# A transformer kernel's first block: who makes the low parts of the weights, and which queue carries the bias tables

## The chip, the core and the metric

The kernel runs on one core of a Trainium2 chip. The metric is the time of one execution in device microseconds (us). A core has TensorE (PE, matrix products), VectorE (DVE), ScalarE (ACT), GpSimd (POOL) and SyncE (SP); each takes its own instructions strictly in their order, and semaphores tie the engines together. Transfers (DMAs) are issued from an engine's queue, and the issuing engine goes on while the data moves.

## What is computed

Two transformer blocks follow each other on a sequence of 512 tokens with 1024 features. All sizes below are of the first block's mixer, which is where the change lies.

```
h = rms_norm(x, norm1_g);  z = h @ w_in
z_pool, s_b, s_c, s_h, c_a, c_g, zq, zk, zv = split(z)
y_pool  = pool_mixer(z_pool)                      # sliding means, then a 64x64 product per group
y_sconv = s_b * causal_dwconv(s_c * s_h)          # 3 taps
u       = causal_dwconv(c_a * sigmoid(c_g)) + b   # 31 taps
y_conf  = silu(layer_norm(u))
y_attn  = diff_attention(zq, zk, zv, rel_bias)    # 4 heads, softmax twice, difference by lambda
x = x + concat(y_pool, y_sconv, y_conf, y_attn) @ w_out
x = x + (silu(h2 @ w_gate) * (h2 @ w_up)) @ w_down
```

Lambda comes from four vectors of 32 numbers: exp(sum(lq1*lk1)) - exp(sum(lq2*lk2)) + a constant. The second block has two more layers with other mixers; its attention uses a second table of relative biases.

## The kernel before

**Products in two parts.** Every large product is made from float32 values that are cut in a high and a low part: `hi` is a rounded copy, `lo = value - hi`. Three products are added up (hi*hi, hi*lo, lo*hi). For activations `feed` (L209 to L220) makes the parts. For weights it is `weights` (from L108): it loads 128x1024 numbers into `wraw` (two buffers) from SyncE's queue (L119), ScalarE casts each half to `whi` (L129), and the engine in `self.lo` subtracts to `wlo` (L130); there are four buffers each of `whi` and `wlo`. L144 (`f_acc`) holds the matmuls with features as output rows, L163 (`t_proj`) those with tokens as output rows. `setup` puts VectorE into `self.lo` (L308); `layer1`, after the first four units of weights, puts GpSimd there (L441), and `run` puts VectorE back after the first block (L1347). In a stretch of the second block (L777 to L856) GpSimd makes lo parts as well; the change leaves that alone.

**The order.** A planner orders the instructions of each engine ahead of time, by priority and by its own estimates. Work under `first()` goes ahead of ordinary work, work under `chain()` ahead of most. The order on each engine is then fixed. A generator list (`bg`) mixes the attention's steps into the matmuls of the projections.

**The first block, in program order.** `setup` (L305) loads the input and constants. `layer1` (L381) makes the parts of the activations and the norm, then calls `tables` (L347): two small matmuls turn the relative biases into rows `t1` (4x640) and `t2` (8x656), and two DMAs write each row 32 times into tables in main memory (`tab1`, `tab2`; L369 and L370). The staging tiles (one-hot rows, mask row, `t1`, `t2`) live in a pool that is closed at the end of `tables`. The memory is then given to the block's own pool, `l1`, and a tile that lies over an older one waits for that one's last user. From SyncE's queue also come the meta rows of `x` (L372), the constants `cs1` (L406), the bias tile `B1` in four pieces read from `tab1` with a shift for each row (`sheared`, L374 to L378), and the pool weights (L413).

Then follow: lambda and scaled gains (L415 to L429, small VectorE instructions and one exponential); the projection `cg` and its sigmoid; the projection `ca`; the product `u = ca * sigmoid(cg)` on VectorE (L444) behind 30 zeros (a memset on GpSimd, L434); the token projections v, k, q (L549 evacuates them on ScalarE); per tile of 128 tokens a chain of norm, split and transposes for k and q (`heads`, L458 to L478, in which VectorE, ScalarE and TensorE alternate); the attention's `logits` (L491 to L502, in which VectorE adds `B1`), `turn`, `values` and `finish`; and the convolution: two VectorE instructions start `y` (L559), 60 more add a tap each (L561). The convolution has ordinary priority. Afterwards come the projections for pooling and the short convolution (L566 to L599), the layer norm of the convolution's result (L608 to L631), and the output product in two halves, the first with the pooling and short convolution, the second with the long convolution and the attention.

Of the kernel before, what the change touches and what calls it, by code (L numbers as in the profile page):

```python
# [8 lines left out]
F32 = mybir.dt.float32  # L9
# [48 lines left out]
class Kern:  # L58
# [246 lines left out]
    def setup(self):  # L305
# [34 lines left out]
            nc.vector.tensor_copy(self.bf[n], self.ident if n == "ident" else k(n))  # L340
        self.m1 = m1

        ps = self.ch("a")
        for _ in range(10):
            nc.tensor.matmul(ps[:, :128], lhsT=m1, rhs=m1, start=True, stop=True)

    def tables(self):  # L347

        nc, io = self.nc, self.io
        self.tab1 = self.dram.tile([4, COPIES, N1], F32, name="tab1")  # L350
        self.tab2 = self.dram.tile([8, COPIES, N2], F32, name="tab2")
        with self.tc.tile_pool(name="setup", bufs=1) as p:
            oh = p.tile([32, N1 + N2], F32, name="oh")
            nc.sync.dma_start(oh, io["onehot"])
            mrow = p.tile([4, N1], F32, name="mrow")
            nc.sync.dma_start(mrow, io["mrow"])
            rb = p.tile([32, 12], F32, name="relb")
            nc.sync.dma_start(rb, io["relb"])
            t1 = p.tile([4, N1], F32, name="t1")
            t2 = p.tile([8, N2], F32, name="t2")  # L360
            for c0, c1 in ((0, 512), (512, N1)):
                ps = self.ch("a")
                nc.tensor.matmul(ps[:4, :c1 - c0], lhsT=rb[:, 0:4], rhs=oh[:, c0:c1], start=True, stop=True)
                nc.vector.tensor_tensor(out=t1[:, c0:c1], in0=ps[:4, :c1 - c0], in1=mrow[:, c0:c1], op=OP.add)
            for c0, c1 in ((0, 512), (512, N2)):
                ps = self.ch("a")
                nc.tensor.matmul(ps[:8, :c1 - c0], lhsT=rb[:, 4:12], rhs=oh[:, N1 + c0:N1 + c1], start=True, stop=True)
                nc.vector.tensor_copy(t2[:, c0:c1], ps[:8, :c1 - c0])
            nc.sync.dma_start(self.tab1, t1[:, None, :].to_broadcast([4, COPIES, N1]))  # L369
            nc.sync.dma_start(self.tab2, t2[:, None, :].to_broadcast([8, COPIES, N2]))  # L370
            for k in range(KT):
                nc.sync.dma_start(self.x[k][:, 0:M], io["meta"][k])  # L372

    def sheared(self, out, tab, n):  # L374

        for p0 in range(0, 128, COPIES):
            src = bass.AP(tensor=tab.tensor, offset=tab.offset + 127 - p0, ap=[[n - 1, COPIES], [COPIES * n, out.shape[1]], [1, out.shape[2]]])
            self.nc.sync.dma_start(out[p0:p0 + COPIES], src)  # L378


    def layer1(self):  # L381
# [10 lines left out]
        with tc.tile_pool(name="l1", bufs=1, reuse_waits="tile") as p:  # L392
# [4 lines left out]
            def fproj(out):  # L397
                for f in range(2):
# [3 lines left out]
                    with self.first():  # L402
                        nc.vector.tensor_tensor(out=out[:, f], in0=ps, in1=rbx, op=OP.mult)

            cs = p.tile([128, NCS1], F32, name="cs1")
            nc.sync.dma_start(cs, self.io["cs1"])  # L406
            B1 = p.tile([128, 4, S], F32, name="B1")
            self.sheared(B1, self.tab1, N1)
            pw = p.tile([128, 2, 128], F32, name="pw")
            nc.gpsimd.memset(pw, 0.0)  # L410
            for g in range(4):
                o = g % 2 * 64
                nc.sync.dma_start(pw[o:o + 64, g // 2, o:o + 64], self.io["pool_w"][g])  # L413

            rp = lambda n: self.rowp[:, ROWS[n][0]:ROWS[n][0] + ROWS[n][1]]  # L415
            lam = p.tile([128, 4], F32, name="lam")
            lt = p.tile([128, 32], F32, name="lt")
            for i in (1, 2):
                nc.vector.tensor_tensor(out=lt, in0=rp(f"lq{i}"), in1=rp(f"lk{i}"), op=OP.mult)
                nc.vector.tensor_reduce(lam[:, i:i + 1], lt, axis=AX.X, op=OP.add)  # L420
            nc.scalar.activation(lam[:, 1:3], lam[:, 1:3], AF.Exp)

            nc.vector.tensor_tensor(out=lam[:, 0:1], in0=lam[:, 2:3], in1=lam[:, 1:2], op=OP.subtract)
            lam_init = 0.8 - 0.6 * math.exp(-0.3 * 0)
            nc.vector.tensor_scalar(lam[:, 0:1], lam[:, 0:1], -lam_init, None, op0=OP.add)
            gq = p.tile([128, 32], F32, name="gq")
            nc.vector.scalar_tensor_tensor(gq, rp("qg"), 32 ** -0.5, rp("kg"), op0=OP.mult, op1=OP.mult)
            gs = p.tile([128, 64], F32, name="gs")
            nc.vector.tensor_scalar(gs, rp("sub"), 1.0 - lam_init, None, op0=OP.mult)  # L429


            PADC = 30
            u = p.tile([128, 2, PADC + S], F32, name="u")
            nc.gpsimd.memset(u[:, :, :PADC], 0.0)  # L434
            ca, cg = X2(S), X2(S)
            fproj(cg)
            with self.chain():
                for f in range(2):
                    self.sigmoid(cg[:, f], cg[:, f])
            fproj(ca)  # L440
            self.lo = nc.gpsimd  # L441
            with self.chain():
                for f in range(2):
                    nc.vector.tensor_tensor(out=u[:, f, PADC:], in0=ca[:, f], in1=cg[:, f], op=OP.mult)  # L444
# [2 lines left out]
            tiles = [(M + 128 * t, 128) for t in range(4)]  # L447
            flat = lambda t: t.rearrange("p f t -> p (f t)").rearrange("p (t c) -> p t c", t=4)
            qt, kt, vt = (flat(G(S, n)) for n in ("qtok", "ktok", "vtok"))
            qT, kT = (p.tile([128, 8, S], F32R, name=n) for n in ("qT", "kT"))  # L450
            yT = G(S, "yT")

            def heads(i, src, dst, b):
# [109 lines left out]

            PADP = 16
            z = G(PADP + S, "z", "ktok")
            nc.gpsimd.memset(z[:, :, :PADP], 0.0)  # L566
            fproj(z[:, :, PADP:])

            PADS = 2
            sb, sc, sh = G(S, "sb", "qtok"), X2(PADS + S), X2(S)  # L570
            nc.gpsimd.memset(sc[:, :, :PADS], 0.0)
            fproj(sc[:, :, PADS:])
            fproj(sh)
            fproj(sb)
# [958 lines left out]
```

## Time and profile before

| | |
|---|---|
| time, median of 3 runs | 1260.43 us (1259.63 to 1261.51) |
| the profiled execution | 1260.34 us, span 1258.5 us |
| TensorE busy | 1212.1 us (96%) |
| VectorE busy | 813.2 us (65%) |
| ScalarE busy | 616.5 us (49%) |
| GpSimd busy | 134.5 us (11%) |
| granted TensorE clock | 0.988 |
| lo parts of weights on VectorE (L130) | 280, 666 ns each in the mean |
| lo parts of weights on GpSimd (L130) | 70, 1382 ns each in the mean |
| taps of the convolution (L561) | 60, 910 ns each in the mean |

In the profile's rows an instruction stands as engine, line, operation, what it writes and reads, its shape and count. A bracket tells how long the engine was idle just before, and what ended the idle time. "Busy" counts instructions only; time in a queue's waits is idle time. TensorE's ends are modelled and overlap a little, so two matmuls of 0.39 us can start 0.23 us apart.

### The profile page before, as it was taken

The numbers are of one execution on the slowest core, as the hardware profiler recorded it, in microseconds if no ns is written. First come the engines' busy times: TensorE is split into PE (matmuls) and PEld (weight loads), VectorE is DVE, ScalarE is ACT, GpSimd is POOL, SyncE is SP. The second block draws the span as 40 slices with busy tenths as digits, with TensorE's granted clock in tenths as the row PEclk, the third lists the DMA queues.
The fourth block names the chain that finished last, engine by engine and source line by source line (L and its number), as shares of the span: only waits on it lengthen the run. The fifth ranks groups of instructions, "written<-read, shape, count | busy, mean of one in ns | idle before, by whom it ended". The sixth has DMA issues, their size and how long they took to land.

```text
span 1258.5 us, 19045 instructions
## 1 busy us (share of the span) xinstructions
PE 1212.1 (96%) x7242; PEld 1023.7 (81%) x7242; DVE 813.2 (65%) x1816; ACT 616.5 (49%) x1367; POOL 134.5 (11%) x108
## 2 busy tenths in 40 slices
PE   8968999999999999999989999999999999999996
PEld 6966767888888888887888889899899989886776
DVE  6499986544433444454498989666566476685675
ACT  5356645433322333344444435666554484575754
POOL 0433336100000000013322000000010000000000
PEclk9989999999999999999998999999999999999999
DMA  6531112233223323233211212222223223120121
GB/s 190 122 80 54 51 51 75 93 100 100 78 90 113 101 89 101 80 92 124 88 51 51 62 49 71 81 69 68 69 68 118 84 68 93 60 82 20 51 67 68
DMA packets 34736, 101.44 MB, mean 81 GB/s; under 512 B 5536, under 2 KB 7984, under 8 KB 34644
## 3 DMA queue, kind: packets, MB, share of 16 engines
q1 hardware_dynamic: 32836, 98.06, 25.7%
q10 hardware_dynamic: 1808, 2.16, 0.5%
q8 instruction: 57, 0.93, 0.3%
q14 instruction: 35, 0.29, 0.1%
HBM read 96.03 MB, written 3.10 MB: 79 GB/s over the span
## 4 chain that ended last, share of the span: by engine, by line
PE 78%; DVE 16%; ACT 2%; DMA 2%; issue 1%; POOL 0%; SPq 0%; DVEq 0%; ACTq 0%; POOLq 0%
PE mm L144 64%; DVE y L561 3%; PE psb L174 3%; DVE sc L817 2%; DVE sc L827 1%; PE pso L1218 1%; DMA tab<-t 1%; DVE m L826 1%; PE pso L971 1%; DVE e L493 1%; DVE mx L103 1%; PE psa L1099 1%; DVE e L502 1%; PE pso L973 1%; DVE wlo L130 1%
## 5 line engine op out<-in xcount | busy, mean ns | idle before, releaser
L144 PE MATMUL mm<-hhi,whi 128*128 128x512 f32 (+3 forms) x1296 | 444.8, 344 | 1.7 <-ACT whi L129 1.6
L144 PE MATMUL mm<-hhi,wlo 128*128 128x512 f32 (+3 forms) x1296 | 437.9, 338 | 0.1
L144 PE MATMUL mm<-hlo,whi 128*128 128x512 f32 (+3 forms) x1296 | 436.2, 337 | 0.2 <-DVE hlo L217 0.2
L129 ACT CAST whi<-wraw 128x512 fp32r<-128x512 f32 x350 | 207.4, 595 | 335.9 <-PE mm L144 289.3
L130 DVE TENSOR_TENSOR wlo<-wraw,whi 128x512 fp32r<-128x512 f32 (+2 forms) x280 | 185.9, 666 | 144.2 <-ACT whi L129 116.8
L144 PEld LDWEIGHTS mm<-hhi,whi 128*128 128x128 f32 (+1 forms) x1296 | 246.0, 190 | 28.1 <-ACT whi L129 2.3
L144 PEld LDWEIGHTS mm<-hhi,wlo 128*128 128x128 f32 (+1 forms) x1296 | 245.7, 190 | 26.7 <-issue 1.2
L144 PEld LDWEIGHTS mm<-hlo,whi 128*128 128x128 f32 (+1 forms) x1296 | 246.0, 190 | 25.6 <-DVE hlo L217 1.5
L130 POOL TENSOR_TENSOR wlo<-wraw,whi 128x512 fp32r<-128x512 f32 (+1 forms) x70 | 96.3, 1382 | 181.9 <-ACT whi L129 171.9
L144 PE MATMUL mm<-mx,whi 128*128 128x512 f32 (+2 forms) x448 | 112.2, 338 | 2.0 <-DVE mx L103 1.6
L231 POOL TENSOR_TENSOR acc<-acc,sq 128x528 f32<-128x528 f32 (+1 forms) x18 | 25.5, 1417 | 610.4 <-PE mm L144 321.7
L144 PEld LDWEIGHTS mm<-mx,whi 128*128 128x128 f32 x448 | 75.5, 189 | 14.1 <-DVE mx L103 3.6
L663 DVE TENSOR_TENSOR gu<-mm,rb 128x512 f32<-128x512 f32 x44 | 30.4, 692 | 71.2 <-PE mm L144 69.4
L144 PE MATMUL mm<-mx,wlo 128*128 128x512 f32 (+2 forms) x224 | 74.4, 333 | 0.0
L144 PE MATMUL mm<-hidh,whi 128*128 128x512 f32 x176 | 68.5, 389 | 0.0
L144 PE MATMUL mm<-hidh,wlo 128*128 128x512 f32 x176 | 68.5, 389 | 0.0
L144 PE MATMUL mm<-hidl,whi 128*128 128x512 f32 x176 | 68.5, 389 | 0.0
L300 DVE TENSOR_TENSOR tmp<-mm,rb 128x272 f32<-128x272 f32 (+2 forms) x76 | 35.7, 470 | 33.1 <-PE mm L144 31.9
L561 DVE SCALAR_TENSOR_TENSOR y<-u,cols,y 128x512 f32<-128x512 f32 x60 | 53.6, 910 | 0.2
L288 DVE TENSOR_TENSOR x<-x,mm 128x272 f32<-128x272 f32 (+2 forms) x72 | 36.7, 510 | 16.4 <-PE mm L144 15.2
L144 PEld LDWEIGHTS mm<-mx,wlo 128*128 128x128 f32 x224 | 42.2, 188 | 3.8 <-issue 0.2
L144 PEld LDWEIGHTS mm<-hidh,whi 128*128 128x128 f32 x176 | 33.0, 188 | 6.9
(394 smaller groups left out, 1843.3 us busy)
## 6 DMA issues: line engine op xcount, KB each, us to landing
wraw<-in_w SPq DMA_DIRECT2D x145, 512.0 KB, 3.5
wraw<-in_w SPq DMA_DIRECT2D x16, 384.0 KB, 3.0
wraw<-in_w SPq DMA_DIRECT2D x16, 320.0 KB, 2.9
bh<-tab SPq DMA_DIRECT2D x16, 132.0 KB, 2.9
mx<-cqk SPq DMA_DIRECT2D x8, 132.0 KB, 2.3
x<-in_x SPq DMA_DIRECT2D x4, 256.0 KB, 4.4
x<-in_x ACTq DMA_DIRECT2D x4, 256.0 KB, 5.6
B<-tab SPq DMA_DIRECT2D x4, 256.0 KB, 6.3
```

The costliest lines, as they stand in the source:

```text
L103: self.nc.vector.tensor_tensor(out=lo, in0=src, in1=hi.bitcast(F32), op=OP.subtract)
L129: self.nc.scalar.copy(hi[:, :w], raw[:, c])
L130: self.lo.tensor_tensor(out=lo[:, :w], in0=raw[:, c], in1=hi[:, :w].bitcast(F32), op=OP.subtract)
L144: nc.tensor.matmul(ps[b], lhsT=ww[i][:, f0:f0 + nf], rhs=aa[:, t0:t1], start=first and i == 0 and j == 0, stop=last and i == n - 1 and j == 2)
L174: self.nc.tensor.transpose(out, in_, self.ident[:n, :n])
L231: e.tensor_tensor(out=acc[:, c0:c1], in0=acc[:, c0:c1], in1=sq[:, c0:c1], op=OP.add)
L288: nc.vector.tensor_tensor(out=x, in0=x, in1=p, op=OP.add)
L300: self.nc.vector.tensor_tensor(out=out[:, t0:t1], in0=p, in1=rb[:nf, t0:t1], op=OP.mult)
L493: nc.vector.tensor_tensor_reduce(out=e, in0=ps[:, :W], in1=B1[:, h, 384 - 128 * i:], scale=-1.0, scalar=BIG, op0=OP.add, op1=OP.min, accum ...
L561: nc.vector.scalar_tensor_tensor(y[:, f], u[:, f, k:k + S], cw[:, f, k:k + 1], y[:, f], op0=OP.mult, op1=OP.add)
L663: nc.vector.tensor_tensor(out=t[:, g], in0=ps, in1=rbx, op=OP.mult)
L817: nc.vector.scalar_tensor_tensor(o, rl, w, o, op0=OP.mult, op1=OP.add)
```

## The change

Five things change together, all in the first block:

- `self.lo` stays VectorE for the whole block, so VectorE makes every `wlo`.
- The tables, the meta rows, `cs1`, `B1` and the pool weights are issued from GpSimd's queue; SyncE keeps the weights.
- `qT` and `kT` are taken from the block's pool ahead of `cs1`, `B1`, `pw` and `u`.
- Lambda and the scaled gains are made in `setup`, in place, in the loaded row tile.
- The three small memsets of the paddings move from GpSimd to VectorE.

```diff
 # setup
+        rp = lambda n: self.rowp[:, ROWS[n][0]:ROWS[n][0] + ROWS[n][1]]
+        lam = self.lam = rp("lq1")[:, 0:4]
+        for i in (1, 2):
+            nc.vector.tensor_tensor(out=rp(f"lk{i}"), in0=rp(f"lq{i}"), in1=rp(f"lk{i}"), op=OP.mult)
+        for i in (1, 2):
+            nc.vector.tensor_reduce(lam[:, i:i + 1], rp(f"lk{i}"), axis=AX.X, op=OP.add)
+        nc.scalar.activation(lam[:, 1:3], lam[:, 1:3], AF.Exp)
+        nc.vector.tensor_tensor(out=lam[:, 0:1], in0=lam[:, 2:3], in1=lam[:, 1:2], op=OP.subtract)
...
 # tables
-            nc.sync.dma_start(self.tab1, t1[:, None, :].to_broadcast([4, COPIES, N1]))
-            nc.sync.dma_start(self.tab2, t2[:, None, :].to_broadcast([8, COPIES, N2]))
+            nc.gpsimd.dma_start(self.tab1, t1[:, None, :].to_broadcast([4, COPIES, N1]))
+            nc.gpsimd.dma_start(self.tab2, t2[:, None, :].to_broadcast([8, COPIES, N2]))
             for k in range(KT):
-                nc.sync.dma_start(self.x[k][:, 0:M], io["meta"][k])
+                nc.gpsimd.dma_start(self.x[k][:, 0:M], io["meta"][k])
 # layer1
+            qT, kT = (p.tile([128, 8, S], F32R, name=n) for n in ("qT", "kT"))
             cs = p.tile([128, NCS1], F32, name="cs1")
-            nc.sync.dma_start(cs, self.io["cs1"])
+            nc.gpsimd.dma_start(cs, self.io["cs1"])
             B1 = p.tile([128, 4, S], F32, name="B1")
-            self.sheared(B1, self.tab1, N1)
+            self.sheared(B1, self.tab1, N1, nc.gpsimd)
...
-                nc.sync.dma_start(pw[o:o + 64, g // 2, o:o + 64], self.io["pool_w"][g])
+                nc.gpsimd.dma_start(pw[o:o + 64, g // 2, o:o + 64], self.io["pool_w"][g])
...
-            nc.gpsimd.memset(u[:, :, :PADC], 0.0)
+            nc.vector.memset(u[:, :, :PADC], 0.0)
...
             fproj(ca)
-            self.lo = nc.gpsimd
...
-            qT, kT = (p.tile([128, 8, S], F32R, name=n) for n in ("qT", "kT"))
...
-            nc.gpsimd.memset(z[:, :, :PADP], 0.0)
+            nc.vector.memset(z[:, :, :PADP], 0.0)
...
-            nc.gpsimd.memset(sc[:, :, :PADS], 0.0)
+            nc.vector.memset(sc[:, :, :PADS], 0.0)
```

More of the change, by code (lines that the diff above doesn't have):

```diff
@@ L341, in setup @@
         self.m1 = m1
+        rp = lambda n: self.rowp[:, ROWS[n][0]:ROWS[n][0] + ROWS[n][1]]
[6 more added lines that the diff above has]
+        nc.vector.tensor_tensor(out=lam[:, 0:1], in0=lam[:, 2:3], in1=lam[:, 1:2], op=OP.subtract)
+        lam_init = 0.8 - 0.6 * math.exp(-0.3 * 0)
+        nc.vector.tensor_scalar(lam[:, 0:1], lam[:, 0:1], -lam_init, None, op0=OP.add)
+        self.gq, self.gs = rp("kg"), rp("sub")
+        nc.vector.scalar_tensor_tensor(self.gq, rp("qg"), 32 ** -0.5, self.gq, op0=OP.mult, op1=OP.mult)
+        nc.vector.tensor_scalar(self.gs, self.gs, 1.0 - lam_init, None, op0=OP.mult)
         ps = self.ch("a")
@@ L368, in tables, with sheared @@
                 nc.vector.tensor_copy(t2[:, c0:c1], ps[:8, :c1 - c0])
-            nc.sync.dma_start(self.tab1, t1[:, None, :].to_broadcast([4, COPIES, N1]))
-            nc.sync.dma_start(self.tab2, t2[:, None, :].to_broadcast([8, COPIES, N2]))
+            nc.gpsimd.dma_start(self.tab1, t1[:, None, :].to_broadcast([4, COPIES, N1]))
+            nc.gpsimd.dma_start(self.tab2, t2[:, None, :].to_broadcast([8, COPIES, N2]))
             for k in range(KT):
-                nc.sync.dma_start(self.x[k][:, 0:M], io["meta"][k])
-    def sheared(self, out, tab, n):
+                nc.gpsimd.dma_start(self.x[k][:, 0:M], io["meta"][k])
+    def sheared(self, out, tab, n, queue=None):
         for p0 in range(0, 128, COPIES):
             src = bass.AP(tensor=tab.tensor, offset=tab.offset + 127 - p0, ap=[[n - 1, COPIES], [COPIES * n, out.shape[1]], [1, out.shape[2]]])
-            self.nc.sync.dma_start(out[p0:p0 + COPIES], src)
+            (queue or self.nc.sync).dma_start(out[p0:p0 + COPIES], src)
     def layer1(self):
@@ L412, in layer1 @@
                 o = g % 2 * 64
-                nc.sync.dma_start(pw[o:o + 64, g // 2, o:o + 64], self.io["pool_w"][g])
[L415 to L429, printed above, removed]
+                nc.gpsimd.dma_start(pw[o:o + 64, g // 2, o:o + 64], self.io["pool_w"][g])
+            lam, gq, gs = self.lam, self.gq, self.gs
             PADC = 30
             u = p.tile([128, 2, PADC + S], F32, name="u")
-            nc.gpsimd.memset(u[:, :, :PADC], 0.0)
+            nc.vector.memset(u[:, :, :PADC], 0.0)
             ca, cg = X2(S), X2(S)
```

## The prediction

> **What bounds the kernel now.** I read the page first, then a table of stages, then the chain of waits, and then the timelines of VectorE and GpSimd inside the stage where TensorE has holes. The page:
>
> ```profile
> span 1258.5 us, 19045 instructions
> ...
> PE   8968999999999999999989999999999999999996
> ...
> DVE  6499986544433444454498989666566476685675
> ...
> POOL 0433336100000000013322000000010000000000
> ```
>
> Each digit stands for 31 us. TensorE (PE) is full nearly everywhere; its holes lie in the first six slices, and there VectorE (DVE) stands at 9 and GpSimd (POOL) is at work. The stages around that place:
>
> ```profile
> 28.00:52.00 24.00, 24.00 (x167) 22.23 (x166) 4.10 (x7) 9.42 (x18) 8.11 (x9) 1.00 0.57 120
> 52.00:182.00 130.00, 109.90 (x623) 89.58 (x621) 127.72 (x297) 75.50 (x204) 49.38 (x34) 0.96 0.22 63
> 182.00:205.00 23.00, 20.58 (x94) 15.39 (x95) 14.51 (x26) 10.77 (x23) 10.88 (x8) 1.00 0.22 69
> ```
>
> The columns are: stretch, its length, then busy time and instructions of PE, its weight loads, DVE, ACT and POOL, the granted clock, the share of DMA and GB/s. From 28 to 52 us VectorE is nearly idle, 4.10 us of 24. From 52 to 182 us it is busy for 127.72 us of 130, while TensorE idles 20.1 us. So one stage is bound by VectorE, and it starts late. The chain of waits says why it starts late and where it ends:
>
> ```profile
> 35.53 15.55 DMA tab<-t
> 51.82 0.68 DVE u L444
> 57.67 8.99 DVE y L561 x9
> ...
> 232.20 267.87 PE mm L144 x1164
> ```
>
> The chain runs through the transfer of the second bias table, into the input of the 31-tap convolution (`u`, L444), through the taps (L561), and then into matmuls without a hole. The taps have nothing to do with that table, yet `u` waits for it:
>
> ```profile
> 32.48 0.69 DVE L403 TENSOR_TENSOR mx<-mm,rb 128x512 f32<-128x512 f32 x1 [2.01 <-PE mm L144]
> 38.02 0.69 DVE L403 TENSOR_TENSOR mx<-mm,rb 128x512 f32<-128x512 f32 x1 [4.85 <-PE mm L144]
> 51.21 1.29 DVE L444 TENSOR_TENSOR u<-mx 128x512 f32<-128x512 f32 x2 [12.50 <-DMA tab<-t]
> 53.93 0.74 DVE L561 SCALAR_TENSOR_TENSOR y<-u,cols,y 128x512 f32<-128x512 f32 x1
> 54.59 1.23 DVE L423 TENSOR_TENSOR lam<-lam 128x1 f32<-128x1 f32 x1
> 55.75 1.86 DVE L561 SCALAR_TENSOR_TENSOR y<-u,cols,y 128x512 f32<-128x512 f32 x1
> ...
> 68.71 1.23 DVE L201 TENSOR_TENSOR rt<-ry 128x8 f32<-128x8 f32 x1
> ...
> 70.60 0.15 DVE L201 TENSOR_TENSOR rt<-ry 128x8 f32<-128x8 f32 x1
> ...
> 180.96 1.18 DVE L561 SCALAR_TENSOR_TENSOR y<-u,cols,y 128x512 f32<-128x512 f32 x1
> ```
>
> Two things are to be seen. VectorE stands still for 12.50 us ahead of `u`: this tile lies where the tables' staging tiles lay, and the transfer that reads them has to end first. And some instructions take far longer than their twins: a tap 1.86 us instead of 0.74, a multiply on 128x8 numbers 1.23 us instead of 0.15. GpSimd runs beside exactly these:
>
> ```profile
> 53.99 6.46 POOL L130 TENSOR_TENSOR wlo<-wraw,whi 128x512 fp32r<-128x512 f32 x4 [2.70 <-ACT whi L129]
> 62.03 1.44 POOL L130 TENSOR_TENSOR wlo<-wraw,whi 128x512 fp32r<-128x512 f32 x1 [1.58 <-PE mm L163]
> 68.22 1.70 POOL L130 TENSOR_TENSOR wlo<-wraw,whi 128x512 fp32r<-128x512 f32 x1 [4.76 <-ACT whi L129]
> ```
>
> **The change part by part.** I keep a ledger of VectorE's time from 38.7 us, when the last product for `u` is there, to about 205 us, where the first block's matmuls close up. What the ledger saves there moves everything behind it, since the matmuls from 232 us on have no holes.
>
> *The wait ahead of `u`.* The two large tiles `qT` and `kT` are now taken first from the block's memory, 16 KB a partition each. The staging pool holds about 13 KB a partition (5.2 for the one-hot rows, and 2.5 or 2.6 for each of the mask row and the two tables), so `qT` alone covers it. `qT` is first written after the heads' work on the last projection, when the tables have long left. So the 12.50 us go. What comes next is the product at 38.02 us, which waits for a matmul. The first half of `u` needs only the product at 32.48, so a part of the 4.85 us ahead of 38.02 opens too; two lo parts of 0.60 us go into it, 3.6 us stay, and I take half, 1.8 us. Bounds: 12.5 to 16.1 us saved; I take 14.3.
>
> *The lo parts.* In the stretch from 28 to 205 us GpSimd makes 40 of them, the first two at 30 and 34 us:
>
> ```profile
> 30.18 1.29 POOL L130 TENSOR_TENSOR wlo<-wraw,whi 128x512 fp32r<-128x512 f32 x1 [29.74 <-ACT whi L129]
> ...
> 33.83 1.29 POOL L130 TENSOR_TENSOR wlo<-wraw,whi 128x512 fp32r<-128x512 f32 x1 [2.31 <-ACT whi L129]
> L130 POOL TENSOR_TENSOR wlo<-wraw,whi 128x512 fp32r<-128x512 f32 x40 | 57.2, 1437 | 112.8 <-ACT whi L129 108.4 <-PE psb L174 2.7 <-PE mm L163 1.6
> L434 POOL MEMSET u<- 128x60 f32 x1 | 0.1, 149 | 4.8 <-DMA tab<-t 4.8
> 9.02 1.29 DVE L130 TENSOR_TENSOR wlo<-wraw,whi 128x512 fp32r<-128x512 f32 x2 [1.24 <-ACT whi L129]
> 25.73 0.69 DVE L130 TENSOR_TENSOR wlo<-wraw,whi 128x512 fp32r<-128x512 f32 x1 [1.08 <-ACT whi L129]
> ```
>
> On VectorE one takes 0.69 us, and the second of two in a row adds 1.29 - 0.69 = 0.60. Two of the 40 fall before 38.7 us; 38 x 0.60 = 22.8 us are added.
>
> *What VectorE gets back.* Taking each instruction's time from its start to the next start, and the usual time of its kind, the instructions that start from 52 to 182 us exceed the usual by 27.3 us in 30 places; the first is the tap at 55.75, the last the one at 180.96. GpSimd runs 34 instructions in that stage, one of them a memset, so 33 with tensor inputs: 27.3 / 33 = 0.83 us each. Of these, five stay (L592 twice, L593, L599 twice) and 28 are lo parts: 28 x 0.83 = 23.2 us come back. The nearest rows bound one of them: a tap loses 1.12 us (1.86 - 0.74) and the one at 180.96 loses 0.44, so 12 to 31 us in all. I take 23.2, since it is the sum over the whole stage. So a lo part on GpSimd costs VectorE as much as making it itself; this part is worth 0.4 us, not the 40 parts of 1.4 us that leave GpSimd.
>
> [...]
>
> *The lambda and the scaled gains.* Eight small VectorE instructions and one exponential leave the place after `u`; six start 0.1 us apart and the one at 54.59 takes 1.16 to the next start, so 1.8 us go. They come before 28 us instead, for 0.8 us, and there VectorE waits for transfers. Their input is loaded by
>
> ```profile
> 7.92 0.33 SPq L328 DMA_DIRECT2D rowp<-in_rows  x1
> ```
>
> and VectorE and ScalarE take them in order. If they stand too early, the low parts of the activations queue behind them and TensorE behind those. I bound this by 0 and 1 us, and take 0.5. Three memsets come from GpSimd to VectorE, 0.15 us at most each: 0.4 us.
>
> *The transfers.* SyncE's queue loses 19 issues (two tables, eight meta rows, the convolution constants, four of `B1`, four of the pool weights), and GpSimd's gets them. On SyncE, the second table stood behind two weight loads:
>
> ```profile
> 24.35 0.30 DVE L368 COPY t<-psa 8x144 f32<-8x144 f32 x1 [0.41 <-PE psa L367]
> 29.25 6.23 SPq L119 DMA_DIRECT2D wraw<-in_w  x2
> 35.53 0.71 SPq L370 DMA_DIRECT2D tab<-t  x1
> 106.35 0.28 DVE L493 CUSTOM_DVE_ANT_0 e<-psa,B 128x128 f32<-128x128 f32 x1
> ```
>
> It was ready at 24.65 and issued at 35.53. On GpSimd it can go at once. The weight loads are behind nothing any more, but from 25 us on they share the DMA engines with both tables at once; TensorE was full from 28 to 52 us beside the same bytes, so I count nothing, and if that cover is gone it is the few us of a load. No issue by GpSimd is in this trace; the nearest rows are an issue on SyncE, 0.71 us, and a GpSimd instruction, 1.44 us. `B1` is wanted at 106.35 us, by the forecast some 15 us earlier. Ahead of its last piece stand at most 15 issues: from 24.65 us on, 15 x 1.44 = 22 us end at 46 us, long before. I count nothing.
>
> [...]
>
> *The sum.* -14.3 (wait) + 22.8 (lo parts) - 23.2 (stretching) - 1.8 + 0.5 (lambda) + 0.4 (memsets) = -15.6 us. The profiled execution took 1260.34 us, with a span of 1258.5, and the median of the runs is 1260.43, so they give 1244.7 and 1244.8; I say 1245. About 0.2%, 2.5 us, is what a measurement of this kernel can tell from no change.
>
> **The rivals.** *TensorE's holes close wholly.* VectorE's ledger only moves the end as far as TensorE has holes: 20.1 us from 52 to 182 and 2.4 from 182 to 205, so 22.5 us. If the stretching falls by the 31 us of the upper bound and all of the early idle time is used, the holes close: 1238. TensorE's modelled ends hide some more room, so it could be 1233. For it speaks that VectorE is full all through the stage; against it, that the heads' chain goes to and fro between engines.
>
> *VectorE waits for what it now has in its queue.* A lo part needs ScalarE's high part first, and VectorE takes its queue in order, so the taps behind it wait as well, and the heads' chain behind those. GpSimd could wait without harm. ScalarE's high parts in this stretch wait for
>
> ```profile
> ACT whi L129 <- DMA wraw<-in_w: 9.2, 3, 5.1
> ACT whi L129 <- PE mm L144: 8.0, 7, 3.0
> ACT whi L129 <- PE mm L163: 3.5, 2, 2.9
> PE psb L174 <- ACT st L469: 12.4, 6, 6.8
> ```
>
> (in total, times, longest). If the 9.2 us for loads fall on VectorE, 1254; with all 20.7 us it would be 1265.5 and slower. Against it: in the first 28 us VectorE made lo parts in this manner and its waits for them are of 1.1 and 1.2 us.
>
> [...]
>
> [...]
>
> *The wait finds another tile.* If `u` or the tile of the taps still lies over the staging tiles, the 14.3 us stay, and the table only leaves earlier: -1.3 us, 1259.
>
> **How the numbers follow.** The forecast, from 1240 to 1250, has 0.55; closed holes 0.15; VectorE's waits for its queue 0.15, of which 0.12 are still faster than before, 0.02 level and 0.01 slower; stretching that stays 0.06; late `B1` 0.04; a wait elsewhere 0.05, level 0.03 and faster by a little 0.02. So faster by over 0.2% is 0.55 + 0.15 + 0.12 + 0.02 = 0.84, within 0.2% 0.05, slower 0.11. The range from 1233 to 1256 holds the forecast, the closed holes and two thirds of the queue's waits, 0.80.
>
> **What would show it.** In the profile after: `u` starts within 2 us of the product before it, with no wait for a table; taps take 0.74 us with few exceptions; GpSimd has some ten tensor instructions left in the first block; TensorE's idle time from 52 us to the end of the block is under 10 us; the matmul run without holes starts near 217 us instead of 232. A VectorE idle time ahead of L130 of over 10 us, logits (L493) that wait for `B1`, or taps that stay at 0.9 us in the mean would make it wrong.

## The result, and the profile after

The change makes the kernel slower: 1273.89 us in the median of 4 runs (1271.46 to 1275.07), against 1260.97 us for the kernel before on the same chip; the ratio is 1.0104 with a 95% interval of 1.0089 to 1.0119. The profiled execution took 1271.46 us, with a span of 1269.5. The forecast was 1245. The page of the kernel after, in the rows shown of before (a digit is 32 us here):

```profile
span 1269.5 us, 19013 instructions
...
PE   8599958999999999999999999999999999999997
...
DVE  6179997644443444444489989766666476685675
...
POOL 2100010200000000002432000000011000000000
```

GpSimd's row has emptied, as the change says. But VectorE's second digit has fallen from 4 to 1 and TensorE's from 9 to 5: the new hole lies between 32 and 63 us, ahead of the stage in which the gain was expected. By stages (columns as in the prediction):

```profile
28.00:52.00 24.00, 16.30 (x97) 14.13 (x95) 3.98 (x7) 5.39 (x10) 1.26 (x2) 0.89 0.67 65
52.00:182.00 130.00, 107.44 (x656) 91.49 (x656) 112.17 (x304) 74.47 (x205) 12.56 (x14) 0.91 0.27 74
```

From 28 to 52 us TensorE was full before; now it works 16.30 us of 24. The DMA engines are busier (0.67 instead of 0.57) and move half as much (65 GB/s instead of 120). The chain of waits names the transfer:

```profile
31.29 25.07 DMA wraw<-in_w
...
57.11 14.63 PE mm L163 x96
```

A weight load of 512 KB takes 25.07 us. These are the rows of ScalarE, of VectorE and of GpSimd around it:

```profile
33.24 0.61 ACT L129 CAST whi<-wraw 128x512 fp32r<-128x512 f32 x1
...
56.44 1.14 ACT L129 CAST whi<-wraw 128x512 fp32r<-128x512 f32 x2 [22.06 <-DMA wraw<-in_w]
...
66.96 1.14 ACT L129 CAST whi<-wraw 128x512 fp32r<-128x512 f32 x2 [6.74 <-DMA wraw<-in_w]
```

```profile
57.09 0.69 DVE L130 TENSOR_TENSOR wlo<-wraw,whi 128x512 fp32r<-128x512 f32 x1 [22.52 <-ACT whi L129]
57.70 0.68 DVE L418 TENSOR_TENSOR mx<-mm,rb 128x512 f32<-128x512 f32 x1
...
67.61 1.29 DVE L130 TENSOR_TENSOR wlo<-wraw,whi 128x512 fp32r<-128x512 f32 x2 [6.59 <-ACT whi L129]
68.83 1.29 DVE L446 TENSOR_TENSOR u<-mx 128x512 f32<-128x512 f32 x2
```

```profile
26.56 0.72 POOL L384 DMA_DIRECT2D tab<-t  x1 [20.89 <-DVE rt L202]
28.03 0.68 POOL L385 DMA_DIRECT2D tab<-t  x1 [0.74 <-DVE t L383]
28.69 0.59 POOL L423 DMA_DIRECT2D cs<-in_cs  x1
52.42 2.21 POOL L393 DMA_DIRECT2D B<-tab  x4 [23.14 <-DMA tab<-t]
```

Read them from the bottom. GpSimd issues both tables at once, at 26.56 and 28.03 us; the first is there only at 52.4. The load, issued behind them, comes as late. ScalarE's cast waits for it, VectorE's lo part waits for the cast, and behind the lo part stand, in VectorE's order, the product for `u` (L418) and `u` itself (L446). So the wait for a table ahead of `u` is gone, as forecast, and yet `u` starts at 68.83 us instead of 51.21.

I kept the prediction's ledger for each kernel: VectorE's time from 38.7 us to the sixteenth add into `x`, where the mixer's output is complete, split in work (each instruction at the lower quartile, for its kind, of the times from its start to the next start), stretching (what goes beyond that) and idle time (from 38.7 us on). The columns add up to the length of the stretch within 1.4 us.

| kernel | median, us | work | stretching | idle | end of block |
|---|---|---|---|---|---|
| before | 1260.97 | 124.2 | 34.7 | 30.0 | 226.3 |
| after | 1273.89 | 147.5 | 12.7 | 43.3 | 240.9 |
| e6, lo parts alone | 1269.12 | 146.9 | 14.0 | 36.7 | 235.5 |
| e8b, after, second table late | 1261.13 | 147.6 | 12.7 | 29.4 | 227.2 |
| e11, and the first from ScalarE | 1248.68 | 144.9 | 12.8 | 19.7 | 215.1 |
| e15, after, tables spread | 1243.92 | 144.3 | 10.6 | 15.8 | 208.4 |
| e16, before, tables spread | 1260.35 | 122.6 | 36.6 | 33.4 | 229.9 |
| e18, e16 and lo parts | 1241.03 | 143.7 | 10.6 | 15.9 | 207.9 |

In the kernel after, work is up by 23.3 us (forecast 22.8) and stretching down by 22.0 (forecast 23.2). Idle time should have fallen, and rose by 13.3.

### The profile page after: what moved, and what is told of

It reads as the page before. It is cut to its first block, busy times and chain, and to the rows that moved or that the text cites. A ratio compares the mean times of both kernels' runs of the same rounds, so it can differ in the third digit from the quotient of the medians.

```text
span 1269.5 us, 19013 instructions
## 1 busy us (share of the span) xinstructions
PE 1211.9 (95%) x7242; PEld 1024.0 (81%) x7242; DVE 816.2 (64%) x1863; ACT 615.3 (48%) x1367; POOL 83.0 (7%) x80
## 4 chain that ended last, share of the span: by engine, by line
PE 83%; DVE 10%; ACT 3%; DMA 3%; issue 1%; POOL 0%; SPq 0%; DVEq 0%; ACTq 0%; POOLq 0%
PE mm L144 66%; PE psb L174 3%; DMA wraw<-in_w 3%; PE mm L163 2%; DVE sc L818 2%; PE pso L1219 1%; DVE sc L828 1%; DVE m L827 1%; DVE y L562 1%; PE pso L972 1%; DVE wlo L130 1%; PE psa L1100 1%; PE pso L974 1%; ACT whi L129 1%; PE psa L1193 1%
## 5 line engine op out<-in xcount | busy, mean ns | idle before, releaser
L130 DVE TENSOR_TENSOR wlo<-wraw,whi 128x512 fp32r<-128x512 f32 x324 | 217.4, 674 | 173.8 <-ACT whi L129 147.8
L300 DVE TENSOR_TENSOR tmp<-mm,rb 128x272 f32<-128x272 f32 (+2 forms) x76 | 35.7, 470 | 29.3 <-PE mm L144 28.1
L562 DVE SCALAR_TENSOR_TENSOR y<-u,cols,y 128x512 f32<-128x512 f32 x60 | 46.4, 781 | 0.4
L288 DVE TENSOR_TENSOR x<-x,mm 128x272 f32<-128x272 f32 (+2 forms) x72 | 36.7, 510 | 14.4 <-PE mm L144 13.2
L163 PE MATMUL mm<-whi,hhi 128*128 128x256 f32 x96 | 28.5, 297 | 13.7 <-ACT whi L129 12.8
L144 PEld LDWEIGHTS mm<-hidh,wlo 128*128 128x128 f32 x176 | 33.0, 188 | 7.0
```

Of the source, the lines that this page charges most:

```text
L130: self.lo.tensor_tensor(out=lo[:, :w], in0=raw[:, c], in1=hi[:, :w].bitcast(F32), op=OP.subtract)
L144: nc.tensor.matmul(ps[b], lhsT=ww[i][:, f0:f0 + nf], rhs=aa[:, t0:t1], start=first and i == 0 and j == 0, stop=last and i == n - 1 and j == 2)
L163: nc.tensor.matmul(part(t), lhsT=aa[:, t0:t0 + nt], rhs=ww[i], start=u + i + j == 0 and t % 2 == 0, stop=u == 1 and i == 3 and j == 2, ski ...
L288: nc.vector.tensor_tensor(out=x, in0=x, in1=p, op=OP.add)
L300: self.nc.vector.tensor_tensor(out=out[:, t0:t1], in0=p, in1=rb[:nf, t0:t1], op=OP.mult)
L562: nc.vector.scalar_tensor_tensor(y[:, f], u[:, f, k:k + S], cw[:, f, k:k + 1], y[:, f], op0=OP.mult, op1=OP.add)
```

## The experiments

Three theories stood at first. **L**: the tables in flight from GpSimd hold the weight loads up. **Q**: lo parts that wait in VectorE's queue cost the time, whatever the tables do. **P**: the pooling's padding memset, which the planner put behind most taps on VectorE (at 172 us), makes the pooling late; TensorE waits there for 11.5 us. In this text "after" and "before" are the two kernels; each edit is to the one named. Medians stand with the ratio to before in the same batch and its interval.

**e1_tables_sync** (after):

```
-            nc.gpsimd.dma_start(self.tab1, ...)
+            nc.sync.dma_start(self.tab1, ...)        # tab2 alike
```

> The changed kernel (1273.9 us) with the two table transfers alone back on SyncE's queue; there one stands ahead of, the other behind, two weight loads. Theory L (the tables' transfers from GpSimd hold a weight load up for 25 us; VectorE and TensorE wait for that load): the load lands within 10 us, VectorE's 22.5 us of idle time ahead of a lo part and TensorE's 7.7 us hole from 28 to 52 us go, u starts before 45 us, and the time falls by 12 to 20 us, to 1254 to 1262. Theory Q (lo parts in VectorE's queue cost the time, whatever the load does): within 4 us of 1273.9. Theory P (the paddings' memsets stand behind the taps, so the pooling is late): the 11.5 us that TensorE waits for the pooling product stay.

1265.81 us, 1.0037 [1.0022, 1.0052]: 8 of the 13 us come back. VectorE's two large waits ahead of lo parts are 4.0 and 12.5 us now; the second is for the load issued behind the second table. L holds in kind, though the time misses its 1254 to 1262, and a load behind a table on SyncE is still late (issued at 43.20 us, it took 15.36).

**e2_memsets_early** (after) and **e3_both** (that, with e1's edit):

```
+            with self.chain():
                 nc.vector.memset(z[:, :, :PADP], 0.0)   # sc's alike
```

> The changed kernel with the memsets of two paddings (pooling and short convolution) still on VectorE, but at the high priority of the chain, so that the planner puts them ahead of the taps. Theory P: TensorE's wait of 11.5 us for the pooling product goes and the time falls by 6 to 12 us, to 1262 to 1268. Theory L: the hole of 7.7 us from 28 to 52 us and VectorE's 22.5 us stay as they are. If the pooling is late only because VectorE as a whole is late, the time stays within 3 us of 1273.9.

> Both edits together. Theories L and P: the gains add up, to 20 to 30 us, so 1244 to 1254, and TensorE's idle time from 52 us to the end of the block is under 12 us; the stretching of VectorE's instructions is gone as well. If the two stalls cover each other, it stands within 4 us of the better one of the two.

1280.23 us, 1.0152 [1.0123, 1.018], and 1270.20, 1.0071 [1.0048, 1.0095]. The 11.5 us wait is gone and both are slower than without the edit, by 6.3 and 4.4 us: the pooling now goes ahead of the taps, and TensorE waits for the last tap instead (11.6 and 10.2 us ahead of the layer norm's matmul). P falls: moving the wait does not make VectorE earlier.

**e4_lo_gpsimd** (after):

```
             fproj(ca)
+            self.lo = nc.gpsimd
```

> The changed kernel with the lo parts given back to GpSimd from the place where they were before. Theory Q: VectorE no longer waits for the load, u starts before 45 us and the time falls under 1262. Theory L: the load is as late as before, TensorE still has a hole of 7 us or more from 28 to 52 us; u comes early, but the taps are stretched again (0.9 us in the mean), and the time lies from 1262 to 1274. GpSimd's lo parts then also stand behind its own wait for the table ahead of B1, which can hold TensorE up further, to 1280.

1267.85 us, 1.0055 [1.0033, 1.0077]. `u` starts at 38.7 and the first tap at 41 us, 13 us ahead of before, and yet the block ends 8.3 us behind it: VectorE then stands 9.9 us ahead of the heads' mean square. This is the first hint that the head start alone is worth nothing. The planner also moved the second table behind GpSimd's lo parts, to 45.8 us, so the run does not separate L from Q.

**e5_u_apart** (before): the allocation of `qT` and `kT` moves up, alone.

```
+            qT, kT = (p.tile([128, 8, S], F32R, name=n) for n in ("qT", "kT"))
             cs = p.tile([128, NCS1], F32, name="cs1")
...
-            qT, kT = (p.tile([128, 8, S], F32R, name=n) for n in ("qT", "kT"))
```

> The kernel before with one part of the change alone: the two operands of heads are allocated ahead of the cosine table, so that u no longer waits for it; lo parts stay on GpSimd, the tables on SyncE, lambda and memsets where they were. Theory L (what the change lost, it lost through the load behind the two tables in flight at once): nothing of that is here, the 12.5 us wait of L444 goes and the end of the first block with it, about 1248 us, first tap near 41 us. Rival O (VectorE's wait for that tile stood in a stretch where the next thing, a weight load behind the second table, is as late, as in the run with lo parts on GpSimd, whose taps began at 41.0 and whose block still ended 8.3 us later than before): the first tap comes at 41 us, a wait of 8 to 12 us for a load's product appears further on, and the time is 1257 to 1263 us.

1259.33 us, 0.9994 [0.9985, 1.0004]: no gain. VectorE's waits from 36 to 62 us, in total, times and longest:

```profile
DVE lam L424 <- ACT lam L422: 7.3, 1, 7.3
DVE y L559 <- POOL u L435: 6.2, 1, 6.2
DVE mx L403 <- PE mm L144: 4.9, 1, 4.9
```

In the place of one wait of 12.5 us stand two of 13.5 in sum, for the padding of `u`, which GpSimd makes behind lo parts, and for lambda's exponential.

**e9_head_start** (before): `u` apart, and lambda (made at the end of `setup`, the change's own lines) and the memset of `u` moved as in the change, so that those two waits go as well.

```
+            qT, kT = (p.tile([128, 8, S], F32R, name=n) for n in ("qT", "kT"))
...
+            lam, gq, gs = self.lam, self.gq, self.gs
...
-            nc.gpsimd.memset(u[:, :, :PADC], 0.0)
+            nc.vector.memset(u[:, :, :PADC], 0.0)
```

> The kernel before with u apart and, besides, the two things that took its place in the run with u apart alone moved as the change moves them: lambda is made in the setup (there VectorE waited 7.3 us for its exponential) and u's padding memset is VectorE's (there 6.2 us for GpSimd's). Lo parts on GpSimd, tables on SyncE, pooling's memsets on GpSimd. Theory H (the head start is real and only those two waits ate it): first tap at 40 to 42 us, no wait of over 4 us on VectorE between 40 and 65 us, block's end about 12 us sooner, 1246 to 1250 us. Rival N (the stretch from 40 to 70 us is paced by TensorE and its weight loads, so VectorE only finds its data missing later): taps start at 41 us, a wait of 7 to 12 us at the mean square of the heads (10 us stood there in the run with lo parts on GpSimd), time 1256 to 1261 us.

1261.23 us, 1.001 [0.9999, 1.0022]. Taps start at 39.9 us, and the third wait in the row appears:

```profile
DVE qss L462 <- ACT qsq L460: 12.9, 1, 12.9
```

The chain of waits in this run goes through two loads, each of them issued while a table is on its way, with lo parts between:

```profile
29.63 11.10 DMA wraw<-in_w
...
44.85 11.19 DMA wraw<-in_w
```

So the stretch from 30 to 65 us is paced by loads behind tables, and a head start of VectorE only moves the place where it waits.

**e6_lo_vector** (before):

```
-            self.lo = nc.gpsimd
```

> The kernel before with the other part alone: VectorE makes all lo parts of the first block, u still waits for the cosine table, the tables stay on SyncE. The working of the prediction: work +22.8, stretching -23.2, the time within 3 us of before. Theory Q (lo parts that wait for their load in VectorE's in-order queue hold everything behind them): the load waits of before, 9.2 us ahead of lo parts, come on top, 1264 to 1271 us, and VectorE shows gaps of 3 us or more ahead of lo parts.

1269.12 us, 1.0069 [1.0043, 1.0094]. Work and stretching cancel (+22.7, -20.7), idle time is 6.7 us up. The number is Q's, the mechanism only in part: VectorE's waits ahead of lo parts come to 3.9 us in all, and its wait for the table ahead of `u` falls from 12.5 to 5.8. TensorE shows where the rest lies. From 28 us to the end of the block, which comes 9.2 us later, it stands 3.3 us more than before (its longest wait, 7.6 us, is for the last tap), and its matmuls take 5.9 us more, at a granted clock of 0.90 instead of 0.97. (The expectation speaks of the cosine table; by the trace `u` waits for a bias table.)

**e7_tables_act** (after, both tables issued by ScalarE) and **e8b_tab2_late** (after, the second table late, by way of a DRAM tile of 8 x 656):

```
-            nc.gpsimd.dma_start(self.tab1, t1[:, None, :].to_broadcast([4, COPIES, N1]))
+            nc.scalar.dma_start(self.tab1, t1[:, None, :].to_broadcast([4, COPIES, N1]))
...
```

```
-            nc.gpsimd.dma_start(self.tab2, t2[:, None, :].to_broadcast([8, COPIES, N2]))
+            nc.gpsimd.dma_start(self.t2d, t2)
...
         a = self.layer1()
+        self.nc.gpsimd.dma_start(self.tab2, self.t2d[:, None, :].to_broadcast([8, COPIES, N2]))
```

> The kernel after with the transfers of both tables issued by ScalarE instead of GpSimd, at nearly the same times: a hardware queue in place of GpSimd's, both still in flight at once. If two tables in flight at once hold the weight load up (theory L, its first form): the load that waits still lands 18 us or more after its issue, and the time is 1270 to 1276 us. If it is GpSimd's queue with its packets of 5 KB and 0.9 to 1.5 us: packets are 2.5 KB and under 0.5 us, the load lands within 12 us of its issue, VectorE's wait ahead of the first lo part is under 10 us instead of 22.5, and the time is 1262 to 1268 us.

> The kernel after, but the second table's rows are first put into a small DRAM tile (8 x 656) and copied out into the 32 shifted copies by a second transfer from GpSimd that is issued behind the first table's reads; so only the first table is in flight when the weight load is issued. Theory L: the load lands within 14 us of its issue, VectorE's wait ahead of the first lo part falls from 22.5 us to under 10, u starts before 55 us, the block ends 8 us or more sooner than in the kernel after: 1256 to 1266 us. If the second table in flight isn't the cause: the wait stays near 20 us and the time at 1271 to 1276 us.

1260.17 us, 1.0004 [0.9995, 1.0013], and 1261.13, 1.0004 [0.9994, 1.0014]: each takes the whole loss away, and nothing but the way of the tables was edited. VectorE's waits ahead of lo parts fall from 22.5 and 6.6 us to 5.2 and 4.1 in the one, to 9.0 and 7.2 in the other. L is shown, by e8b most plainly, where every number that it named came. In e7 the second table's packets begin at 33.3 us, beside the first's, which run until 40.1, but 190 of the 256 begin only after that. The loads issued at 33.3 and 44.5 us took 15.6 and 14.7 us, less than the 18 of one theory and more than the 12 of the other, and the time lies below the bands of both.

**e11_act_tab2** (after): e8b's edit, and

```
-            nc.gpsimd.dma_start(self.tab1, t1[:, None, :].to_broadcast([4, COPIES, N1]))
+            nc.scalar.dma_start(self.tab1, t1[:, None, :].to_broadcast([4, COPIES, N1]))
-            nc.gpsimd.dma_start(self.t2d, t2)
+            nc.scalar.dma_start(self.t2d, t2)
```

> The kernel after with both mendings of its transfers together: the first table issued by ScalarE's queue, the second copied out late by GpSimd. If the loads behind the tables are all that the change lost, each mending has already taken nearly all of it (1260.2 and 1261.1) and the two together bring at most the rest of VectorE's waits ahead of lo parts, 16 and 9 us there: 1250 to 1260 us. If the change's remaining loss lies at the end of the block (pooling and the taps in VectorE's queue), 1258 to 1262 us.

1248.68 us, 0.9922 [0.9902, 0.9941], 11 us faster than before and just below the first band. No wait of VectorE ahead of a lo part is over 2.4 us, the first tap is at 37.4 us.

**e10_head_tab2** (e9 with the late second table), **e12_lo_back** (e11 with lo parts on GpSimd again) and **e13_before_route** (before with e11's transfers) were to tell which part earns this. The line in e12 is

```
             fproj(ca)
+            self.lo = nc.gpsimd
```

and in e13, beside e11's lines for the tables, the other setup transfers of before move to GpSimd (the meta rows and pool weights as well):

```
-            nc.sync.dma_start(cs, self.io["cs1"])
+            nc.gpsimd.dma_start(cs, self.io["cs1"])
-            self.sheared(B1, self.tab1, N1)
+            self.sheared(B1, self.tab1, N1, nc.gpsimd)
...
```

> The kernel with the head start (label e9_head_start), and the second table copied out late through a small DRAM tile, on SyncE, so that no weight load before about 60 us stands behind it. Theory N (loads pace the stretch): weights land sooner, the wait at the heads' mean square shrinks by what the second table took, some 5 to 10 us, time 1247 to 1255 us. Theory H: nothing was left to gain there, the same as the run without it within 3 us.

> The kernel with both mendings (1248.7), but GpSimd makes the lo parts of the first block again. The prediction's ledger holds lo parts at -0.4 in all, so 1248 to 1252 us by it. Rival S (lo parts on GpSimd cost more than their stretching, since TensorE then waits on a lo part that shares its engine with DMA issues and is made at 1.4 us beside VectorE's work): 1255 to 1266 us, as in the run with the late second table on SyncE (1266.9).

> The kernel before with the transfers of the mended kernel alone (first table from ScalarE, second late from GpSimd through the small DRAM tile, the other setup transfers from GpSimd), lo parts on GpSimd, u, lambda and memsets as before. If the way of the tables earns the gain by itself: 1246 to 1252 us. If it takes the lo parts off GpSimd too: 1257 to 1266 us.

1266.88 us, 1.0064 [1.0043, 1.0085]; 1281.69, 1.0167 [1.015, 1.0184]; 1292.84, 1.0254 [1.0236, 1.0272]. All three are slower, and for a reason that the expectations had not named. With the lo parts on GpSimd and the second table late, the planner lets the taps go first: the last tap ends at 136.5, 91.2 and 104.9 us. It ends at 171 in e11, and at 181 to 188 in before, e4, e5 and e9, whose lo parts are on GpSimd too, but whose second table is early. In e12 and e13 the heads' chain is queued behind the taps, and TensorE behind the heads; in e12:

```profile
PE psb L174 <- ACT st L472: 33.1, 3, 30.8
```

In e10 TensorE's waits are many and short (5.3 us in all for the longest kind). So e12 and e13 price an order, not the lo parts, and in both GpSimd's lo parts also share a queue with ten DMA issues. They settle nothing about the terms.

**e14_no_apart** (e11, with `qT` and `kT` back behind `u`, e5's lines the other way round):

> The kernel with both mendings (1248.7), but the allocation that sets u apart is undone. Since the second table's source is now read out in a small transfer, the bytes that u takes over come free early in any case: theory, the same within 2 us, 1247 to 1251. Rival (u waits for the first table's transfer, done near 39 us, or for the cosine table): u later by 5 to 12 us and the time 1252 to 1260 us.

1252.17 us, 0.9941 [0.9924, 0.9957]: 3.5 us more than e11. `u` waits 7.2 us, for the small transfer `t2d` (20.5 KB in 10.13 us, from 31.97 to 42.10), issued behind the first table on ScalarE's queue, which is there at 41.2 us; half of that wait reaches the end.

**e15_spread** (after), **e16_before_spread** (before) and **e17_head_spread** (e9). The same bytes in the tables, with the 32 copies as the slowest dimension instead of the 4 or 8 rows:

```
-            nc.gpsimd.dma_start(self.tab1, t1[:, None, :].to_broadcast([4, COPIES, N1]))
+            nc.gpsimd.dma_start(t1d, t1)
+            nc.gpsimd.dma_start(self.tab1.rearrange("f c n -> c f n"), t1d[None].to_broadcast([COPIES, 4, N1]))
```

> The kernel after, but each table is first written as 4 (or 8) rows into a small DRAM tile and copied from there with the 32 copies as the slowest dimension, still from GpSimd and both early. Theory F (few engines: the table's 4 or 8 rows keep its packets on 4 or 8 of the 16 DMA engines, and the loads wait for those): the copies are done within 6 us each, the weight load lands within 8 us of its issue instead of 25, VectorE's waits ahead of lo parts fall under 8 us in all, and the time is 1244 to 1250 us. Rival G (GpSimd's queue itself starves the loads, however the transfer is cut): load 15 us or more, 1258 us or more.

> The kernel before with the same two small DRAM tiles and the copies as the slowest dimension, from SyncE, nothing of the change. If the way of the tables earns the gain by itself (u's wait for the second table goes here too, since its staging tile is read out in a small transfer): 1246 to 1252 us. If lo parts on VectorE are needed for it: 1256 to 1262 us.

> The kernel before with the head start (u apart, lambda early, u's memset on VectorE) and the tables' copies as the slowest dimension, from SyncE; lo parts on GpSimd. By the prediction's ledger (lo parts -0.4 in all) it should come within 2 us of the kernel after with the same transfers: 1244 to 1252 us. Rival (with VectorE free early, the planned order puts the taps ahead of the heads, as in the runs whose taps were done by 91 and 137 us): 1260 us or more, taps done before 140 us.

e15: 1243.92 us, 0.9874 [0.9857, 0.9892], at the lower end of F's band. The two loads issued behind the tables in the kernel after and in e15 (both from 30 to 40 us), and the tables' own transfers (after from 26 to 60 us, e15 from 24 to 57), with KB each and the median time to landing:

```profile
wraw<-in_w SPq DMA_DIRECT2D x2, 512.0 KB, 24.7
...
tab<-t POOLq DMA_DIRECT2D x1, 656.0 KB, 25.7
tab<-t POOLq DMA_DIRECT2D x1, 320.0 KB, 25.6
```

```profile
wraw<-in_w SPq DMA_DIRECT2D x2, 512.0 KB, 7.7
...
tab<-t2d POOLq DMA_DIRECT2D x1, 656.0 KB, 5.0
tab<-t1d POOLq DMA_DIRECT2D x1, 320.0 KB, 3.8
```

The same two loads take 6.7 and 8.8 us instead of 25.1 and 24.4, with both tables still early and still from GpSimd; the loads after them, with no table in flight, take 3.3 to 3.5. G falls, and F's times hold (the second load is a little over its 8 us); on which DMA engines the packets ran is not shown, since the trace does not number the engines. VectorE in e15, around `u`:

```profile
32.99 0.69 DVE L450 TENSOR_TENSOR u<-mx 128x512 f32<-128x512 f32 x1
33.60 0.68 DVE L130 TENSOR_TENSOR wlo<-wraw,whi 128x512 fp32r<-128x512 f32 x1
34.20 0.65 DVE L564 TENSOR_SCALAR y<-u,cols 128x512 f32<-128x512 f32 x1
34.89 0.75 DVE L566 SCALAR_TENSOR_TENSOR y<-u,cols,y 128x512 f32<-128x512 f32 x1
37.73 0.69 DVE L130 TENSOR_TENSOR wlo<-wraw,whi 128x512 fp32r<-128x512 f32 x1 [2.10 <-PE mm L144]
```

But e16 and e17, with GpSimd's lo parts, stay at 1260.35, 1.0008 [0.9998, 1.0018], and 1260.09, 1.0005 [0.9994, 1.0017]. Fast tables alone earn nothing, with or without the head start.

**e18_lo_spread** (e16, with the lo parts on VectorE and nothing else of the change):

```
-            self.lo = nc.gpsimd
```

> The kernel before with the tables' copies as the slowest dimension, from SyncE (label e16_before_spread, 1260.35), and one part of the change: VectorE makes the lo parts of the first block. If the lo parts on VectorE, fed in time, earn the gain: 1243 to 1250 us, taps spread to 150 us and later. If the gain needs GpSimd's queue for the tables or the early lambda as well: 1254 us or more.

1241.03 us, 0.9847 [0.9823, 0.9871]: 19.3 us less than e16 by this one line, the fastest of all. What it brings is to be seen from 52 to 110 us, in e16 and in e18:

```profile
52.00:110.00 58.00, 42.88 (x280) 39.10 (x280) 55.87 (x109) 29.05 (x81) 18.28 (x13) 0.85 0.23 70
```

```profile
52.00:110.00 58.00, 55.11 (x366) 48.15 (x366) 57.79 (x160) 41.00 (x117) 2.76 (x3) 1.00 0.29 88
```

VectorE is full in both. In e16 it makes taps at 0.91 us each, 60 of them by 105 us, while TensorE waits for the heads; in e18 it gets through 160 instructions instead of 109, and TensorE works 12 us more, at a granted clock of 1.00 instead of 0.85. The tap groups, of e16 and of e18, have the means:

```profile
L565 DVE SCALAR_TENSOR_TENSOR y<-u,cols,y 128x512 f32<-128x512 f32 x60 | 52.4, 910 | 0.1
```

```profile
L564 DVE SCALAR_TENSOR_TENSOR y<-u,cols,y 128x512 f32<-128x512 f32 x60 | 43.3, 746 | 0.2
```

## Why the prediction was wrong, by its own steps

**The transfers: the step that failed.** "I count nothing, and if that cover is gone it is the few us of a load." It put at nothing a term that is not a few us but 30: the kernel after with its tables spread takes 1243.92 us, against 1273.89 (two batches, whose kernel before differs by 1.5). The prediction argued that TensorE was full from 28 to 52 us beside the same bytes. The bytes were the same, their place in time was not. Before, the first table ran from 23.4 to 36.2 us and the second from 38.0 to 50.8, by their packets, and a load could pass between them. In the kernel after both ran at once from 29.3 to 51.8 us, and the second until 53.3. What was missed is that the cover had a length. The trace of before shows the load of 29.25 us land at 38.74, 9.5 us later, with one table in flight; ScalarE's cast of it follows:

```profile
38.82 1.14 ACT L129 CAST whi<-wraw 128x512 fp32r<-128x512 f32 x2 [5.06 <-DMA wraw<-in_w]
```

TensorE had matmuls on earlier weights for that time, and so it was full. In the kernel after it had them until 44.3 us (57.11 less the 12.82 us that it stood), 13 us from the issue of the load; the load took 25. The prediction had named the sign, a VectorE idle time ahead of L130 of over 10 us; it is 22.5.

**The queue rival had a mechanism that took place, at the wrong price.** It said that lo parts waiting for loads would hold up what stands behind them in VectorE's queue, from 9.2 to 20.7 us. Both bounds came from the loads' waits in the trace of before, and the change alters those very waits: VectorE's total in the kernel after is

```profile
DVE wlo L130 <- ACT whi L129: 30.8, 4, 22.5
```

So it was given 0.01 for a slower kernel. It should have been joined to the transfers: one moves the tables in front of the loads, the other makes VectorE wait for the loads, and without the first such waits are small: 3.9 us in e6, with the old transfers, so that e6's loss (+9.3 us, 1269.12 against 1259.83) is not the queue's alone. Giving the lo parts of the kernel after back to GpSimd (e4, where the second table goes out later as well) brings 6 us, the transfers 30.

**The wait ahead of `u`, -14.3.** The row went as forecast, but the term was wrong as a term of its own: without the lo parts it is worth nothing, -0.5 us in e5 and +1.2 in e9 (in e17 against e16, -0.3, `u` has no such wait either way). With the lo parts on VectorE, a wait of 7.2 us ahead of `u` costs 3.5 us (e14 against e11). What is late next was named as the matmul behind the product, 3.6 us; in fact it was the padding memset, lambda's exponential and then the heads' mean square.

**The lo parts, +22.8, and the stretching, -23.2.** Both sizes were right, +23.3 and -22.0 (with line and tile in what counts as a kind, +20.4 and -19.1). "A lo part on GpSimd costs VectorE as much as making it itself; this part is worth 0.4 us" was right for VectorE's busy time and wrong for the time of the kernel. With loads in time it is worth 19.3 us (e18 against e16, in which the order of the taps changes too), and there VectorE's idle time falls as well, by 17.5 us, and the heads come sooner; with the old transfers it costs 9.3 us (e6).

**The sum.** With the transfers mended e15 lies 15.6 us under before, and the sum was -15.6. VectorE's idle time is 14.2 us down there, and the forecast for the wait was 14.3. So the ledger was a fair forecast of VectorE's time, but that it meets the kernel's time to the digit is luck: e15's block ends 17.9 us sooner, and the ledger has no term for the granted clock. Nor did the forecast get the parts right: e18 reaches the same ledger without setting `u` apart, since with a short transfer out of the staging tiles `u` has nothing to wait for.

**The other rivals.** Stretching that stays (it fell from 34.7 to 12.7 us), and a wait elsewhere for `u`'s tile, did not happen. `B1` was late only as its table was: it could be issued at 52.42 us, and no logits waited for it. The issues themselves were cheap: in e15 the four of `B1`, beside the VectorE rows above, take 0.55 us each.

```profile
32.85 2.20 POOL L397 DMA_DIRECT2D B<-tab  x4 [2.28 <-DMA tab<-t1d]
```

**What stays open.** Why the gain of the lo parts exceeds VectorE's busy time by so much is read from the traces, not isolated: with lo parts between them the taps end at 162 us and fill gaps, without them they are over by 105 and VectorE waits in pieces of 1 to 2 us. A run that fixes the order of the taps and changes the lo parts' engine alone was not made. TensorE's side gives a part of it: from 28 us to the block's end it stands 24.5 us in e16 and 8.9 in e18, which is 15.6 of the 22.0 us, and the other 6.4 are its matmuls, which take 177.4 and 171.0 us, at granted clocks of 0.94 and 0.99. In the same way 11.4 of the 14.6 us by which the block of the kernel after ends later are TensorE's standing and 3.2 its matmuls (clock 0.91 instead of 0.97). No run holds the clock fixed. And e15 changes two things about the tables, the number of rows that stand outermost (32 instead of 4 or 8) and the source (main memory instead of a few rows on chip); e8b and e11 separate them for the second table only, as the last section shows.

## What to carry to other kernels

The tables moved to a queue that was idle, and the loads on another queue were still held up: 25.07 us for one, against 3.3 to 3.5 with no table in flight (e15). Before counting such a move at nothing, look in the trace at what the loads beside the transfer do while it runs, and how long it is for its bytes. When a change puts a wait into an in-order queue, price that wait in the world after the change, with the transfers where the change puts them, not from the trace before. And a wait that ends on a paced stretch is only worth what the next one leaves: three waits were removed here one after another for nothing, until the pace itself was mended and the lo parts had moved.

## What the runs showed of the hardware

**While a table of few rows ran, a part of each load waited.** The first table's 320 KB took 12.8 us before (23.4 to 36.2), at 26 GB/s. Never more than 4 of its packets ran at one time, 3.7 in the mean, and in after, e7, e8b and e11 it was 4 at most as well (3.6 to 3.7); of the second's 656 KB, in 8 rows, it was 7.1 in the mean, 9 at most (one over, but packets overlap a little in the record: the loads' packets, for which the page counts 16 DMA engines, stand at up to 19). Of a load's 128 packets of 4 KB, issued at 29.25 us, 96 started by 32 us and the other 32, a quarter of them, only from 35.9 us on, as the table ended. A quarter is 4 of the 16 DMA engines, as many as the table had packets at one time; that a load is spread evenly and its quarter waits for the engines that the table holds is my estimate from these counts, since the trace does not number the engines. In the kernel after, of the 256 packets of two loads 32 had started by 34 us, and the last 128 started only from 51 us on. In e15, with 32 outermost, up to 19 of a table's packets run at one time, and both tables are out in 7.3 us (26.7 to 34.0).

**The packets that read a few rows on chip took longer than those from main memory.** The first table's packets of 5120 bytes took, in the median, 0.78 us each from GpSimd's queue with no other table beside (e8b), 1.48 with the second table beside (after), and 0.20 when they were read from main memory (e15, with 32 outermost). The second table tells the source from the number of rows. With 8 rows outermost it took 12.7 us from the chip, alone and from SyncE (before), 24.0 us from the chip, beside the first table and from GpSimd (after), and 5.1 us from main memory, from GpSimd (e8b, 46.4 to 51.5); with 32 outermost and from main memory it took 2.5 us (e15). So in these runs the source brings more than the number of rows. The two loads issued behind the table in e8b still took 8.1 and 7.7 us.
